# A decoder trunk on one core: stores of tiles that ScalarE wrote last go out from ScalarE's own queue

## The chip, the cores and the metric

The kernel runs on one core of a Trainium2 chip. The metric is the device time of one execution in microseconds, as a median of several executions. A profiled execution has its own time, and the span of its trace runs from the first instruction to the last.

## The reference, cut to what matters

One layer of a decoder for 2048 tokens of width 1024. A mixer whose one input projection is split between a gated linear attention group (GLA, 4 heads) and an RWKV-7 group (8 heads with a recurrent state), one output projection, and then a gated MLP with a causal convolution:

```python
h = modulate(x, norm_mix_g[l], sh_m, sc_m)
proj = h @ w_proj
o_gla = gla_group(proj[..., :GLA_COLS], ...)
o_rwkv, v_first = rwkv7_group(proj[..., GLA_COLS:], ...)
mixed = jnp.concatenate([o_gla, o_rwkv], axis=-1) @ w_out[l]
x = x + gt_m[:, None, :] * mixed
h = modulate(x, norm_ffn_g[l], sh_f, sc_f)
x = x + gt_f[:, None, :] * conv_ffn(h, ffn_up[l], ffn_conv_w[l], ffn_conv_b[l], ffn_down[l])
return rms_norm(x, final_g)
```

## The kernel before

Tokens are cut into 4 blocks of 512. Everything is float32, and a large product is made of three passes over operands split into a high and a low part (`hi`, `lo`): that is what lines 281 to 283, 352 to 354 and 450 to 452 do.

The **first part** of the program (to about 1410 us) is the mixer. Two streams of work are interleaved in it. One is the recurrence, 16 units of 128 tokens: `rwkv_p` prepares a unit, `rwkv_i` and `rwkv_j` invert a small triangular matrix, `rwkv_s` advances the state in two steps, `gla` does the other head group. In a step PE multiplies (L991), ScalarE copies the result out of PSUM to `p1s` (L994), PE multiplies (L999), ScalarE copies to `rw_uv` (L1002), PE multiplies again (L1009). The other stream is filler: `stage_b` makes the input projection of the next block, and `spare` makes the output projection. It gives PE something to do while the recurrence waits.

The **second part** is the MLP, a long run of products (L1268 to L1270 and L1325 to L1327). No transfer of it is touched.

The order on each engine's queue is not the order of the code. The framework schedules the recorded instructions against its own model of their durations, by priority, and then fixes one in-order stream for each engine: PE, DVE, ACT, POOL and SP. Every transfer takes one of eight completion semaphores in turn (`DMAHW0` to `DMAHW7`), over all queues together, and waits until the transfer that had it before, eight transfers earlier, has landed. So a new issuing queue changes what the scheduler does with all five streams.

Transfers to DRAM in the first part, all of them issued by SP before:

- `Weights` (L197 to L202): a weight half is loaded to `w_st`, ScalarE casts it to `w_hi` (L190), DVE or POOL forms `w_lo` (L193). Both are kept in DRAM as `khi` and `klo`, and loaded again for later blocks (L179).
- `evacuate` (L328 to L339): ScalarE copies a projection from PSUM to `ev`; for t of TZ and above, DVE and POOL then add the shifted tokens, and ScalarE saves the last column in `carry` (L338), which is also the last read of the PSUM bank. L339 stores `ev` in `proj`. There are two banks (`g_bank`) for the filler.
- `values_tok` (L360), the branch for TZ (L389) and block 0's first tiles (L587, L589) store tiles that ScalarE copied.
- `rwkv_p` (L864): ScalarE writes `rw_mab` (L855), which goes to DRAM as `inv_a` and comes back in another layout as `rw_ln` (L866) for DVE in `rwkv_i`.

Of the kernel before, what the change touches and what calls it, by code (L numbers as in the profile page):

```python
# [9 lines left out]
F32 = mybir.dt.float32  # L10
# [19 lines left out]
TQ, TK, TV, TG, TZ, TR, TRK, TRV, TWA, TPG = 0, 2, 4, 8, 12, 13, 17, 21, 25, 26  # L30
# [65 lines left out]
def hybrid_kernel(ctx, tc, x, cst, vec, c_row, ada_t, w_in, w_v, w_first, w_z, gk_up, wa_up, g_up,  # L96
                  w_out, ffn_up, ffn_down, out, T=2048):
# [68 lines left out]
    class Weights:  # L166

        def __init__(self, src, split=True, cols=1024, key=None, at=0, keep=True):
            n = pools["np"]
            step = 1024 // n  # L170
            self.step = step
            self.st, self.hi, self.lo = [], [], []
            for i in range((cols + step - 1) // step):
                w = min(step, cols - i * step)
                if split and (key, at + i) in kept:
                    pair = []
                    for s_, from_ in zip(("hi", "lo"), kept[key, at + i]):
                        t = pools["w"].tile([P, step], F32R, name="w_" + s_, tag="w" + s_, bufs=pools["nhl"])
                        nc.sync.dma_start(out=t.bitcast(F32), in_=from_)  # L179
                        pair.append(t)  # L180
                    self.hi.append(pair[0])
                    self.lo.append(pair[1])
                    continue
                t = pools["w"].tile([P, step], F32, name="w_st", tag="wst", bufs=pools["nst"])
                nc.sync.dma_start(out=t[:, 0:w], in_=src[:, i * step:i * step + w])
                self.st.append(t)
                if split:
                    hi = pools["w"].tile([P, step], F32R, name="w_hi", tag="whi", bufs=pools["nhl"])
                    lo = pools["w"].tile([P, step], F32R, name="w_lo", tag="wlo", bufs=pools["nhl"])
                    A.copy(out=hi[:, 0:w], in_=t[:, 0:w])  # L190
                    split_n[0] += 1
                    eng = G if split_n[0] % 3 == 0 else V
                    eng.tensor_tensor(out=lo[:, 0:w], in0=t[:, 0:w], in1=hi[:, 0:w].bitcast(F32), op=ALU.subtract)  # L193
                    self.hi.append(hi)
                    self.lo.append(lo)
                    if key is not None and keep:
                        to = []  # L197
                        for s_, t in (("hi", hi), ("lo", lo)):
                            d_ = dram.tile([P, step], F32, name=f"k{s_}_{len(kept)}")
                            nc.sync.dma_start(out=d_, in_=t.bitcast(F32))  # L200
                            to.append(d_)
                        kept[key, at + i] = to  # L202

# [89 lines left out]
    def dst_of(b, t):  # L293
        for t0, n in groups:
            if t0 <= t < t0 + n:
                return pd[b][t0][:, t - t0, :]
# [31 lines left out]
    def evacuate(b, t, ps):  # L328
        ev = ap.tile([P, NB], F32, name="ev", tag="ev", bufs=pools["nev"])
        if t < TZ:  # L330
            A.activation(out=ev, in_=ps, func=AF.Copy, scale=0.125 if t < TK else 1.0)
        else:

            m = t - TR
            A.activation(out=ev, in_=ps, func=AF.Copy, scale=omu[:, m:m + 1])
            V.scalar_tensor_tensor(out=ev[:, 1:NB], in0=ps[:, 0:NB - 1], scalar=vcol("mu", m), in1=ev[:, 1:NB], op0=ALU.mult, op1=ALU.add)
            G.tensor_tensor(out=ev[:, 0:1], in0=ev[:, 0:1], in1=carry[:, m:m + 1], op=ALU.add)
            A.activation(out=carry[:, m:m + 1], in_=ps[:, NB - 1:NB], func=AF.Copy, scale=vcol("mu", m))  # L338
        nc.sync.dma_start(out=dst_of(b, t), in_=ev)  # L339

    def values_tok(b, h, i):

        bks = [gbank(), gbank()]
        for c in range(2):
            w = Weights(w_v[i, c], key=("v", i, c), keep=b + 1 < NBLK)
            parts_ = [(k, t) for k in range(4) for t in range(4)] if c == 0 else [(k, t) for p_ in range(2) for k in range(4) for t in (2 * p_, 2 * p_ + 1)]
            for k, t in parts_:
                tc.cur_priority += step[0] // 4
                wh, wl = w.pair(k * 256, 256)
                hi, lo = (a_[:, t * P:(t + 1) * P] for a_ in h[4 * c + k])  # L350
                o_ = bks[t // 2][:, (t % 2) * 256:(t % 2) * 256 + 256]
                PE.matmul(out=o_, lhsT=hi, rhs=wh, start=c == 0 and k == 0 and t % 2 == 0, stop=False)
                PE.matmul(out=o_, lhsT=lo, rhs=wh, start=False, stop=False)
                PE.matmul(out=o_, lhsT=hi, rhs=wl, start=False, stop=c == 1 and k == 3 and t % 2 == 1)
            if c == 0:
                yield
        for p_ in range(2):
            ev = ap.tile([P, NB], F32, name="ev", tag="ev", bufs=pools["nev"])
            A.copy(out=ev, in_=bks[p_])
            nc.sync.dma_start(out=pd[b][TV][:, 2 * p_:2 * p_ + 2, i * 256:(i + 1) * 256], in_=ev.rearrange("p (t c) -> p t c", t=2))  # L360
        yield

    def stage_b(b):

        h = ahead.pop(b)[1]
        order = ([TZ] + list(range(8, TZ)) if b == 0 else list(range(8)) + [TZ] + list(range(8, TZ))) + [TWA, TPG] + [TR + i for i in range(12)]
        for i_, t in enumerate(order):
            if b + 1 < NBLK:
                if i_ == len(order) - 15:
                    ahead[b + 1] = stats_a(b + 1)  # L370
                if i_ == len(order) - 11:
                    stats_b(b + 1)
                if i_ == len(order) - 7:
                    stage_a(b + 1, range(0, EXTRA))
                if i_ == len(order) - 2:
                    stage_a(b + 1, range(EXTRA, KT))
            if t == TZ:

                ps = gbank()
                w = Weights(w_z, split=False, cols=KT * 32)  # L380
                for i in range(2):
                    for p_ in range(2):
                        for j in range(4):
                            k = 4 * i + j
                            PE.matmul(out=ps[32 * j:32 * j + 32], lhsT=w.cut(w.st, k * 32, 32), rhs=h[k][p_].bitcast(F32),
                                      start=i == 0 and p_ == 0, stop=i == 1 and p_ == 1)
                ev = ap.tile([P, NB], F32, name="ev", tag="ev", bufs=pools["nev"])
                A.activation(out=ev, in_=ps, func=AF.Identity, bias=vcol("zone"))
                nc.sync.dma_start(out=pd[b][TZ][:, 0, :], in_=ev)  # L389
                yield  # L390
                continue
            if TV <= t < TG:
                if (t - TV) % 2 == 0:
                    yield from values_tok(b, h, (t - TV) // 2)
                continue
            if b > 0 and i_ < 2:
                if i_ == 0:
                    bks = pair_gemm(w_in, 0, "in", h, b + 1 < NBLK)
                ps = bks[i_]
            elif b + 1 < NBLK and i_ >= len(order) - 2:  # L400
                if i_ == len(order) - 2:
                    bks = pair_gemm(w_in, t - 1, "in", h, b + 1 < NBLK)
                ps = bks[i_ - len(order) + 2]
            else:
                ps = gbank()
                t_ = t if t < TZ else t - 1
                gemm3(ps, Weights(w_in[t_], key=("in", t_), keep=b + 1 < NBLK), h)
            evacuate(b, t, ps)
            yield

# [169 lines left out]
    for i, t in enumerate((TQ, TK, TV, TV + 2)):  # L580
        hv, t_ = halves(i, "p0")
        dst = pd[0][min(t, TV)]
        o_ = t - min(t, TV)
        for j in range(2):
            A.activation(out=hv[j], in_=banks[2 * i + j], func=AF.Copy, scale=0.125 if t == TQ else 1.0)
            if t_ is None:
                nc.sync.dma_start(out=dst[:, o_ + j], in_=hv[j])  # L587
        if t_ is not None:
            nc.sync.dma_start(out=dst[:, o_:o_ + 2], in_=t_)  # L589
    ahead[0] = (rb, h0)  # L590
    nc.sync.dma_start(out=ct, in_=cst[:, P:c0])

# [177 lines left out]
    def rwkv_p(b, q, n):  # L770
# [90 lines left out]
        md = dram.tile([2, 8, 4 * 1040], F32, name="inv_a", tag="inv_a", bufs=2)  # L861
        ln = ctile([64, 16, 16], F32, name="rw_ln", tag="rw_ln", bufs=1)
        for par in range(2):
            nc.sync.dma_start(out=md[par, :, 0:4096].rearrange("a (p t) -> p a t", t=64), in_=mv[pars[par]])  # L864
        for par in range(2):
            nc.sync.dma_start(out=ln[par * 32:par * 32 + 32],  # L866
                              in_=md[par].rearrange("a (b y) -> (a b) y", b=4)[:, 0:1024].rearrange("l (s t) -> l s t", t=64)[:, :, 0:16])
# [703 lines left out]
```

## Time and profile before

| | |
|---|---|
| median of 3 runs | 2934.18 us (2933.49 to 2939.03) |
| profiled execution | 2927.03 us, span 2925.2 us |
| PE busy | 2751.4 us, 94% of the span |
| DVE, ACT, POOL busy | 71%, 44%, 37% |
| mean granted TensorE clock | 0.961 |
| transfers | 486.91 MB, 166 GB/s on average |

A profiled execution is one execution: its own time stands 7 us below the median of the others. PE is busy nearly all the time, so what matters is the time in which it waits, and the stretches in which the clock granted to it is below 1.00.

### The profile page before, as it was taken

Reading aid. Unit: us, or ns where it says so; the run is one execution under the profiler, and the core shown is the slowest. Engines: PE = TensorE matmul, PEld = TensorE weight load, DVE = VectorE, ACT = ScalarE, POOL = GpSimd, SP = SyncE. Lnnn points to the kernel's source line nnn. Section 1 sums busy time; section 2 is a strip of 40 time slices with the busy share of each in tenths; the row PEclk is TensorE's granted clock in tenths of the full one; section 3 lists DMA queues with packets and bytes.
Section 4 is the critical chain, followed back from the end, with each engine's and each line's share of the span. In section 5 each row is a group of like instructions: output and inputs, shape, how many; then the busy total and the mean of one; then the engine's idle time right before and its main releaser. Section 6 shows DMA issues by size and latency. Waiting matters only on the chain.

```text
span 2925.2 us, 54728 instructions
## 1 busy us (share of the span) xinstructions
PE 2751.4 (94%) x20296; PEld 2229.9 (76%) x20296; DVE 2085.8 (71%) x4103; ACT 1298.4 (44%) x2721; POOL 1088.3 (37%) x1150
## 2 busy tenths in 40 slices
PE   6989999999999999999779999999997999999998
PEld 5767777877787777778557888888776788888887
DVE  8356977656676667886687685776868786685867
ACT  4444345444444446443354353442534444353443
POOL 5213222312221223332456363553436454363541
PEclk9999999999999999889789999999998999999999
DMA  8989945645545566546314425234564624425243
GB/s 287 352 288 312 280 139 178 191 143 159 171 150 154 163 196 206 164 124 213 120 43 162 141 87 166 87 126 149 185 227 144 209 94 129 138 90 162 88 130 110
DMA packets 363532, 486.91 MB, mean 166 GB/s; under 512 B 80769, under 2 KB 153729, under 8 KB 363265
## 3 DMA queue, kind: packets, MB, share of 16 engines
q1 hardware_dynamic: 363264, 483.41, 51.9%
q8 instruction: 160, 2.62, 0.4%
q14 instruction: 108, 0.88, 0.1%
HBM read 342.77 MB, written 140.51 MB: 165 GB/s over the span
## 4 chain that ended last, share of the span: by engine, by line
PE 69%; DVE 13%; DMA 9%; ACT 3%; issue 3%; POOL 2%; SPq 0%; DVEq 0%; POOLq 0%; ACTq 0%
PE g_bank L1270 9%; PE g_bank L1268 9%; PE g_bank L1269 9%; PE g_bank L1325 5%; PE g_bank L1327 5%; PE g_bank L1326 5%; PE g_bank L281 4%; PE g_bank L283 4%; PE g_bank L282 4%; PE gl_bank L698 1%; DMA rw_k<-proj 1%; DMA acc<-acc 1%; PE g_bank L450 1%; DMA w_st<-in_ada_t 1%; PE g_bank L452 1%
## 5 line engine op out<-in xcount | busy, mean ns | idle before, releaser
L1268 PE MATMUL g_bank<-h_hi,w_hi 128*128 128x512 f32 x1232 | 488.0, 396 | 26.6 <-ACT h_hi L1143 14.8
L1269 PE MATMUL g_bank<-h_lo,w_hi 128*128 128x512 f32 x1232 | 487.3, 396 | 12.7 <-DVE h_lo L1165 6.8
L1270 PE MATMUL g_bank<-h_hi,w_lo 128*128 128x512 f32 x1232 | 479.7, 395 | 9.7 <-POOL w_lo L1144 7.8
L1143 ACT CAST w_hi<-w_st 128x512 fp32r<-128x512 f32 (+1 forms) x396 | 238.6, 607 | 487.4 <-PE g_bank L1326 348.4
L1328 DVE SCALAR_TENSOR_TENSOR acc<-g_bank,mod,acc 128x512 f32<-128x512 f32 (+1 forms) x200 | 144.7, 728 | 249.7 <-PE g_bank L1327 230.7
L1144 POOL TENSOR_TENSOR w_lo<-w_st,w_hi 128x512 fp32r<-128x512 f32 x154 | 219.3, 1425 | 241.7 <-ACT w_hi L1143 237.9
L281 PE MATMUL g_bank<-h_hi,w_hi 128*128 128x512 f32 x736 | 299.0, 406 | 8.0 <-DMA w_hi<-khi 3.8
L1268 PEld LDWEIGHTS g_bank<-h_hi,w_hi 128*128 128x128 f32 x1232 | 235.1, 191 | 81.6 <-ACT h_hi L1143 18.0
L282 PE MATMUL g_bank<-h_lo,w_hi 128*128 128x512 f32 x736 | 294.9, 401 | 0.0
L283 PE MATMUL g_bank<-h_hi,w_lo 128*128 128x512 f32 x736 | 294.9, 401 | 0.0
L1269 PEld LDWEIGHTS g_bank<-h_lo,w_hi 128*128 128x128 f32 x1232 | 235.0, 191 | 64.1 <-DVE h_lo L1165 8.2
L1270 PEld LDWEIGHTS g_bank<-h_hi,w_lo 128*128 128x128 f32 x1232 | 234.9, 191 | 63.3 <-POOL w_lo L1144 12.3
L1325 PE MATMUL g_bank<-hh,w_hi 128*128 128x512 f32 x640 | 251.9, 396 | 6.0 <-DVE acc L1328 6.0
L1326 PE MATMUL g_bank<-hl,w_hi 128*128 128x512 f32 x640 | 251.6, 395 | 0.0
L1327 PE MATMUL g_bank<-hh,w_lo 128*128 128x512 f32 x640 | 251.6, 395 | 0.0
L1144 DVE TENSOR_TENSOR w_lo<-w_st,w_hi 128x512 fp32r<-128x512 f32 (+1 forms) x242 | 201.6, 833 | 15.2 <-ACT w_hi L1143 10.5
L281 PEld LDWEIGHTS g_bank<-h_hi,w_hi 128*128 128x128 f32 x736 | 140.3, 191 | 41.6 <-issue 4.5
L283 PEld LDWEIGHTS g_bank<-h_hi,w_lo 128*128 128x128 f32 x736 | 140.1, 190 | 30.8 <-DMA w_lo<-klo 0.7
L282 PEld LDWEIGHTS g_bank<-h_lo,w_hi 128*128 128x128 f32 x736 | 140.6, 191 | 28.0 <-issue 0.2
L1325 PEld LDWEIGHTS g_bank<-hh,w_hi 128*128 128x128 f32 x640 | 120.1, 188 | 37.3 <-DVE acc L1328 6.9
L1327 PEld LDWEIGHTS g_bank<-hh,w_lo 128*128 128x128 f32 x640 | 120.2, 188 | 29.4
L1326 PEld LDWEIGHTS g_bank<-hl,w_hi 128*128 128x128 f32 x640 | 120.2, 188 | 29.1
(342 smaller groups left out, 6108.7 us busy)
## 6 DMA issues: line engine op xcount, KB each, us to landing
acc<-acc SPq DMA_DIRECT2D x352, 256.0 KB, 3.1
w_hi<-khi SPq DMA_DIRECT2D x188, 256.0 KB, 3.5
w_lo<-klo SPq DMA_DIRECT2D x188, 256.0 KB, 3.8
w_st<-in_ffn_up SPq DMA_DIRECT2D x176, 256.0 KB, 2.9
proj<-ev SPq DMA_DIRECT2D x100, 256.0 KB, 3.5
w_st<-in_ffn_down SPq DMA_DIRECT2D x80, 256.0 KB, 2.7
khi<-w_hi SPq DMA_DIRECT2D x68, 256.0 KB, 3.8
klo<-w_lo SPq DMA_DIRECT2D x68, 256.0 KB, 3.9
```

The costliest lines, as they stand in the source:

```text
L281: PE.matmul(out=ps, lhsT=wh, rhs=hi, start=k == 0, stop=False)
L282: PE.matmul(out=ps, lhsT=wh, rhs=lo, start=False, stop=False)
L283: PE.matmul(out=ps, lhsT=wl, rhs=hi, start=False, stop=k == KT - 1)
L1143: A.copy(out=hi, in_=t)
L1144: eng.tensor_tensor(out=lo, in0=t, in1=hi.bitcast(F32), op=ALU.subtract)
L1268: PE.matmul(out=ps, lhsT=wh[:, c], rhs=hi, start=first and k == 0, stop=False, skip_group_check=True)
L1269: PE.matmul(out=ps, lhsT=wh[:, c], rhs=lo, start=False, stop=False, skip_group_check=True)
L1270: PE.matmul(out=ps, lhsT=wl[:, c], rhs=hi, start=False, stop=last and k == 3, skip_group_check=True)
L1325: PE.matmul(out=ps, lhsT=wh, rhs=hh, start=j == 0, stop=False)
L1326: PE.matmul(out=ps, lhsT=wh, rhs=hl, start=False, stop=False)
L1327: PE.matmul(out=ps, lhsT=wl, rhs=hh, start=False, stop=j == n - 1)
L1328: V.scalar_tensor_tensor(out=a_, in0=ps, scalar=mod[:, 40 + ft:41 + ft], in1=a_, op0=ALU.mult, op1=ALU.add)
```

## The change

Of the stores above, 149 are issued from ScalarE's queue: 68 `khi` halves, 28 projections with t below TZ, 12 of `values_tok`, 4 of TZ, 5 first tiles of block 0, and 32 of `inv_a`. SP keeps 68 `klo` halves, 56 projections with t of TZ and above, and all loads. The same bytes go to the same places.

```diff
--- before.py
+++ after.py
@@ -197,7 +197,7 @@
                         to = []
                         for s_, t in (("hi", hi), ("lo", lo)):
                             d_ = dram.tile([P, step], F32, name=f"k{s_}_{len(kept)}")
-                            nc.sync.dma_start(out=d_, in_=t.bitcast(F32))
+                            (A if s_ == "hi" else nc.sync).dma_start(out=d_, in_=t.bitcast(F32))
                             to.append(d_)
                         kept[key, at + i] = to
 
@@ -336,7 +336,7 @@
             V.scalar_tensor_tensor(out=ev[:, 1:NB], in0=ps[:, 0:NB - 1], scalar=vcol("mu", m), in1=ev[:, 1:NB], op0=ALU.mult, op1=ALU.add)
             G.tensor_tensor(out=ev[:, 0:1], in0=ev[:, 0:1], in1=carry[:, m:m + 1], op=ALU.add)
             A.activation(out=carry[:, m:m + 1], in_=ps[:, NB - 1:NB], func=AF.Copy, scale=vcol("mu", m))
-        nc.sync.dma_start(out=dst_of(b, t), in_=ev)
+        (A if t < TZ else nc.sync).dma_start(out=dst_of(b, t), in_=ev)
 
     def values_tok(b, h, i):
 
@@ -357,7 +357,7 @@
         for p_ in range(2):
             ev = ap.tile([P, NB], F32, name="ev", tag="ev", bufs=pools["nev"])
             A.copy(out=ev, in_=bks[p_])
-            nc.sync.dma_start(out=pd[b][TV][:, 2 * p_:2 * p_ + 2, i * 256:(i + 1) * 256], in_=ev.rearrange("p (t c) -> p t c", t=2))
+            A.dma_start(out=pd[b][TV][:, 2 * p_:2 * p_ + 2, i * 256:(i + 1) * 256], in_=ev.rearrange("p (t c) -> p t c", t=2))
         yield
 
     def stage_b(b):
@@ -386,7 +386,7 @@
                                       start=i == 0 and p_ == 0, stop=i == 1 and p_ == 1)
                 ev = ap.tile([P, NB], F32, name="ev", tag="ev", bufs=pools["nev"])
                 A.activation(out=ev, in_=ps, func=AF.Identity, bias=vcol("zone"))
-                nc.sync.dma_start(out=pd[b][TZ][:, 0, :], in_=ev)
+                A.dma_start(out=pd[b][TZ][:, 0, :], in_=ev)
                 yield
                 continue
             if TV <= t < TG:
@@ -584,9 +584,9 @@
         for j in range(2):
             A.activation(out=hv[j], in_=banks[2 * i + j], func=AF.Copy, scale=0.125 if t == TQ else 1.0)
             if t_ is None:
-                nc.sync.dma_start(out=dst[:, o_ + j], in_=hv[j])
+                A.dma_start(out=dst[:, o_ + j], in_=hv[j])
         if t_ is not None:
-            nc.sync.dma_start(out=dst[:, o_:o_ + 2], in_=t_)
+            A.dma_start(out=dst[:, o_:o_ + 2], in_=t_)
     ahead[0] = (rb, h0)
     nc.sync.dma_start(out=ct, in_=cst[:, P:c0])
 
@@ -861,7 +861,7 @@
         md = dram.tile([2, 8, 4 * 1040], F32, name="inv_a", tag="inv_a", bufs=2)
         ln = ctile([64, 16, 16], F32, name="rw_ln", tag="rw_ln", bufs=1)
         for par in range(2):
-            nc.sync.dma_start(out=md[par, :, 0:4096].rearrange("a (p t) -> p a t", t=64), in_=mv[pars[par]])
+            A.dma_start(out=md[par, :, 0:4096].rearrange("a (p t) -> p a t", t=64), in_=mv[pars[par]])
         for par in range(2):
             nc.sync.dma_start(out=ln[par * 32:par * 32 + 32],
                               in_=md[par].rearrange("a (b y) -> (a b) y", b=4)[:, 0:1024].rearrange("l (s t) -> l s t", t=64)[:, :, 0:16])
```

The scheduler then orders all engines anew. Three places show what that looks like.

The **sync queue**, where a unit's `inv_a` goes out while the filler loads kept weights (`w_hi<-khi`, `w_lo<-klo`). Before:

```order
L780 DMA rw_pg<-proj_26_100 128x128
L339 DMA proj_26_110<-ev 128x512
L1047 DMA mix_113<-rw_yq 128x4x128
L864 DMA inv_a<-rw_mab 64x8x64 x2
L866 DMA rw_ln<-inv_a 32x16x16 x2
L179 DMA w_hi<-khi_1191 128x512
L179 DMA w_lo<-klo_1193 128x512
```

With the change:

```order
L780 DMA rw_pg<-proj_26_100 128x128
L339 DMA proj_26_110<-ev 128x512
L1047 DMA mix_113<-rw_yq 128x4x128
L866 DMA rw_ln<-inv_a 32x16x16
L179 DMA w_hi<-khi_1191 128x512
L866 DMA rw_ln<-inv_a 32x16x16
L179 DMA w_lo<-klo_1193 128x512
```

The two stores are gone; the two loads of `rw_ln`, which need them landed, keep their places among the loads of weights.

**ScalarE**, about where the last projections of block 0 are evacuated and block 1's first weights are cast (`w_hi_1812` and `w_hi_1822` are the same halves in both). Before:

```order
L338 ACTIVATE carry_137<-g_bank_1453,vt_66 128x1
L190 CAST w_hi_1812<-w_st_1810 128x512
L190 CAST w_hi_1822<-w_st_1820 128x512
L682 COPY gl_kt_3010<-gl_bank_3011 128x256
L335 ACTIVATE ev_1549<-g_bank_1504,omu_139 128x512
L338 ACTIVATE carry_137<-g_bank_1504,vt_66 128x1
```

With the change:

```order
L338 ACTIVATE carry_137<-g_bank_1453,vt_66 128x1
L190 CAST w_hi_1812<-w_st_1810 128x512
L200 DMA khi_36_1816<-w_hi_1812 128x512
L704 COPY atf_658<-gl_bank_3108 64x64
L705 COPY atf_658<-atd0_659 64x2x64
L706 COPY atf_658<-atd0_659 64x2x64
L190 CAST w_hi_1822<-w_st_1820 128x512
L335 ACTIVATE ev_1549<-g_bank_1504,omu_139 128x512
L200 DMA khi_37_1826<-w_hi_1822 128x512
L338 ACTIVATE carry_137<-g_bank_1504,vt_66 128x1
```

A store now stands behind each cast, and `khi_37` stands between the copy `ev_1549` and the `carry` that ends the reading of its bank.

**PE**, in one step of the recurrence near its end (`rs_bank_14603` is written by L999, and L1009 needs ScalarE's copy of it in `rw_uv`). Before:

```order
L281 MATMUL g_bank_14182<-h_hi_13632,w_hi_14195 128x512
L282 MATMUL g_bank_14182<-h_lo_13633,w_hi_14195 128x512
L999 MATMUL rs_bank_14603<-p1s_656,yf1_655 64x64 x4
L690 MATMUL gl_bank_14417<-gl_d_14261 32x32 x2
L698 MATMUL gl_bank_14417<-gl_d_14261 64x64 x10
L698 MATMUL gl_bank_14417<-gl_qk_14163 64x64 x2
L699 MATMUL gl_bank_14417<-gl_d_14261 64x64
L999 MATMUL rs_bank_14603<-p1s_656,yf1_655 64x64 x4
L283 MATMUL g_bank_14182<-h_hi_13632,w_lo_14196 128x512
L281 MATMUL g_bank_14182<-h_hi_13638,w_hi_14195 128x512
```

33 more rows stand there before L1009 of that step, 17 of them of L281 to L283. With the change:

```order
L452 MATMUL g_bank_13651<-h_hi_13644,w_lo_13700 128x512
L450 MATMUL g_bank_13652<-h_hi_13644,w_hi_13709 128x512
L451 MATMUL g_bank_13652<-h_lo_13645,w_hi_13709 128x512
L452 MATMUL g_bank_13652<-h_hi_13644,w_lo_13710 128x512
L999 MATMUL rs_bank_14603<-p1s_656,yf1_655 64x64 x8
L1009 MATMUL rs_bank_14614<-rw_uv_14569,rw_bkt_13149 64x64 x8
L851 MATMUL rp_bank_14058<-rw_t_14040,rw_bk_14041 128x128 x4
L852 MATMUL rp_bank_14059<-rw_t_14040,rw_bk_14041 128x128 x4
```

L1009 follows L999 at once.

## Rows read from the trace of the kernel before

**Rows 1.** Page, part 1: busy time of each engine, us (share of span), instructions.
```profile
PE 2751.4 (94%) x20296; PEld 2229.9 (76%) x20296; DVE 2085.8 (71%) x4103; ACT 1298.4 (44%) x2721; POOL 1088.3 (37%) x1150
```

**Rows 2.** Windows: each engine's busy us (instructions), granted clock, DMA share, GB/s.
```profile
0.00:1440.00 1440.00, 1340.98 (x14130) 1082.71 (x14130) 984.51 (x2723) 663.73 (x1656) 397.67 (x516) 0.95 0.64 201
...
200.00:420.00 220.00, 195.37 (x1885) 160.56 (x1883) 170.42 (x489) 91.75 (x229) 61.43 (x68) 0.92 0.81 258
...
1100.00:1300.00 200.00, 187.51 (x2111) 150.52 (x2102) 163.53 (x467) 102.20 (x273) 67.12 (x83) 0.87 0.54 166
...
1410.00:1500.00 90.00, 49.05 (x216) 35.70 (x216) 70.42 (x85) 38.16 (x64) 52.85 (x41) 0.70 0.29 88
```

**Rows 3.** Page, part 4: the chain that ended last, by engine.
```profile
PE 69%; DVE 13%; DMA 9%; ACT 3%; issue 3%; POOL 2%; SPq 0%; DVEq 0%; POOLq 0%; ACTq 0%
```

**Rows 4.** Waits of the sync queue, 0 to 1440 us: total us, times, longest.
```profile
SPq L179 <- PE g_bank L283: 130.0, 72, 12.9
...
SPq L864 <- ACT rw_mab L855: 39.4, 14, 7.8
...
SPq L200 <- ACT w_hi L190: 26.7, 22, 3.2
...
SPq L866 <- DMA inv_a<-rw_mab: 22.7, 21, 2.8
...
SPq L360 <- ACT ev L359: 12.5, 6, 5.2
...
SPq L339 <- ACT ev L331: 8.2, 8, 2.2
...
SPq L200 <- ACT atf L704: 6.6, 3, 2.9
```

**Rows 5.** Waits of PE, 0 to 1440 us: total us, times, longest.
```profile
PE g_bank L450 <- ACT carry L338: 12.3, 3, 8.3
...
PE rs_bank L1009 <- ACT rw_uv L1002: 2.4, 1, 2.4
...
PE rp_bank L113 <- DMA rw_v<-proj: 1.2, 2, 0.6
```

**Rows 6.** Issues of the stores by line: ns minimum/median/maximum, first and last start.
```profile
L200 SPq DMA_DIRECT2D khi<-w_hi x68: 319/382/1697, 71.8 to 1170.2; - x68
...
L339 SPq DMA_DIRECT2D proj<-ev x84: 319/332/1227, 94.1 to 1097.0; - x84
...
L360 SPq DMA_DIRECT2D proj<-ev x12: 370/374/992, 264.7 to 894.5; - x12
...
L589 SPq DMA_DIRECT2D proj<-p x3: 407/821/1006, 77.0 to 81.4; - x3
...
L864 SPq DMA_DIRECT2D inv_a<-rw_mab x32: 595/615/625, 269.2 to 1324.2; - x32
```

**Rows 7.** Timeline, ACT then PE, 207 to 213 us: start, us, instruction [idle before].
```profile
207.72 1.27 ACT L335 ACTIVATE ev<-g_bank,omu 128x512 f32<-128x512 f32 x2
212.19 0.62 ACT L190 CAST w_hi<-w_st 128x512 fp32r<-128x512 f32 x1 [3.20 <-DMA w_st<-in_w_in]
212.71 0.41 ACT L338 ACTIVATE carry<-g_bank,vt 128x1 f32<-128x1 f32 x2
...
213.02 0.79 PE L450 MATMUL g_bank<-h_hi,w_hi 128*128 128x512 f32 x1 [8.28 <-ACT carry L338]
```

**Rows 8.** Timeline, ACT then PE, about 1403 us.
```profile
1403.77 0.75 ACT L1002 COPY rw_uv<-rs_bank 64x256 f32<-64x256 f32 x2 [4.43 <-PE rs_bank L999]
...
1403.04 0.69 PE L999 MATMUL rs_bank<-p1s,yf 128*64 128x64 f32 x16
...
1403.99 0.39 PE L450 MATMUL g_bank<-h_hi,w_hi 128*128 128x512 f32 x1
1404.22 0.40 PE L451 MATMUL g_bank<-h_lo,w_hi 128*128 128x512 f32 x1
```

## Prediction

> **What bounds the kernel now.** I read the page from the top. The share of busy time [rows 1] comes first: TensorE (PE) works in 94% of the span, ScalarE in 44%. A change that touches neither the number nor the length of matmuls can only move PE's idle time and the clock it is granted. The chain that ended last [rows 3] says who stands between matmuls: VectorE 13%, transfers 9%, ScalarE 3%, and the sync engine's own queue (SPq) 0%. So the issuing of transfers is nowhere on the path as a whole.
>
> Next the windows [rows 2], since the change is in the first part alone. Over 0 to 1440 us PE is idle for 99.0 us (1440 less 1341.0). Three stretches hold most of what can move: 200 to 420 us, where the transfers are dense (DMA share 0.81) and PE idles 24.6 us at clock 0.92; 1100 to 1300 us, 12.5 us idle at 0.87; and the passage to the second part, 1410 to 1500 us, 41.0 us idle at 0.70. A clock of 0.87 over 200 us means work of 26 us lost to the lower of the two levels (13% of 200), so that stretch loses 38.5 us in all.
>
> Then the waits of the two queues that the change touches. SP [rows 4] waits longest for PE (130.0 us at L179, a reload of weights that needs a free buffer), which the change leaves alone. For ScalarE's tiles, ahead of stores that now leave SP, it waits 39.4 us at L864, 26.7 and 6.6 us at L200, 12.5 us at L360 and 8.2 us at L339: 93.4 us. PE's own waits [rows 5] say whether that hurts: for a load it waits 1.2 us at L113; for ScalarE 12.3 us, three times, at L450 (a bank that `carry` has not finished reading) and 2.4 us once at L1009. In 1440 us PE hardly waits for a late transfer, and does wait for a late ScalarE.
>
> **What the change removes, adds and moves.** 149 issues move from SP to ScalarE; bytes and destinations stay.
>
> *Term A, issuing on ScalarE.* The price of an issue is taken from SP's rows [rows 6], since before ScalarE issues none of these stores: 68 `khi` at 0.382 us make 26.0; 28 + 4 at 0.332 (L339's form) 10.6; 12 at 0.374 4.5; 5 at 0.821 4.1; 32 `inv_a` at 0.615 19.7. That adds 64.9 us to ScalarE's queue, 5% to its 1298.4 us. It is nothing if all of it lies in ScalarE's idle time (it works 663.7 of the first 1440 us), and 64.9 us if ScalarE is always what PE waits for. The nearest row is ScalarE's share of the chain: 3% of 2925.2 us is 88 us, 6.8% of its 1298.4 busy us. I price the issues alike: 64.9 x 0.068 = **+4.4 us**. Queued behind them are the evacuations (L331 to L338, L359), the casts and the copies to `p1s` and `rw_uv`; PE waits for all of these.
>
> *Term B, relief of SP.* Not all 93.4 us of waits vanish. Behind each `khi` stands `klo`, made from `w_hi` by another engine later, so SP waits there for it instead; behind `inv_a` stands the load of `rw_ln`, which needs the store landed (L866 waits 22.7 us for it already [rows 4]). What goes for good is L360 and L339, 20.7 us, and the issue time. Bounds: 0, since the queue has 0% of the chain and PE waits 1.2 us for such loads, to -20.7. I stay near the chain's row and take **-2 us**.
>
> The Trainium skill, DMA: Bandwidth & Descriptors, section "Issuing engines are not separate DMA queues", says that transfers started by any engine run on the same 16 DMA engines, and that spreading the issuing saves only the sequencer's time, usually small. By it B would be 0 and the sum below 2 us higher. The DMA share of 0.81 in 200 to 420 us [rows 2] agrees that the shared part is what is loaded there.
>
> *Term C, shorter cover in the recurrence.* The order is made anew. Between L999 and L1009 stands a ScalarE copy; [rows 8] show its length: L999 starts at 1403.04 and takes 0.69, the copies start at 1403.77 and end 0.75 later, 0.79 us after L999's end, or about 1.0 us after its last matmul's start. Meanwhile PE needs other work, at 0.23 us a big matmul (1403.99 to 1404.22). Counting the work between such pairs over all 16 units, the order before falls short of 1.0 us once, by 0.1 us. With the change L1009 falls short six times, with 0.7, 0.8, 0.6, 0.2, 0.2 and 0.5 us of cover, and L999 once behind `p1s`, with 0.9: 3.0 + 0.1 = 3.1 us. Less the 0.1 of before, **+3 us**; 0 if the streams are elsewhere late enough to hide it, 6 if the clock falls to the lower level in these gaps and doubles it.
>
> *Term D, the passage to the second part.* With the change the last step of the recurrence, some 4 us of small products, is mixed with the first matmuls of the MLP (L1268), where before the last projection matmuls covered it. That is work for a stretch with 41.0 us of idle PE [rows 2], but VectorE, busy 70.4 of its 90 us, has that step's work to do as well. Bounds -4 and +4 by those 4 us; I take **-1 us**.
>
> *Clock and the spread of filler.* The filler matmuls between successive units move: from unit 12 on, 103, 119 and 105 stand between one L880 and the next, where it was 93, 74 and 73. I set this at 0 in the sum, since more filler there means less elsewhere, and treat it as a rival.
>
> **Sum:** 4.4 - 2 + 3 - 1 = +4.4 us on the profiled 2927.0 us, so 2931.4. That execution stands 7 us below the median of the runs, so the difference is carried to the median: 2934.2 + 4 = **2938 us**. A measurement of this kernel tells about 0.2%, 5.9 us, from nothing, so this forecast is near its own limit of detection.
>
> **Rivals.**
>
> *1. ScalarE's queue blocks in order (slower).* In front of each store the queue must wait until its completion semaphore, used eight transfers earlier, is free, and on ScalarE everything behind waits too. [rows 7] show what one such hold costs: a cast waits 3.20 us for `w_st`, the `carry` behind it is late, and PE stands idle for 8.28 us and goes on at 0.79 us a matmul, where 0.39 is the rule [rows 8]. With the change `khi` stores stand at just this place, and about half of the 68 fall before 420 us. In the other direction, SP's issue of `khi` took up to 1.697 us against a median of 0.382 [rows 6]. If two more holds of that size arise, 16.6 us take the place of the 4.4 of term A, and the sum is +16.6: about 2951 us. It decides from one hold on, if it is longer than the filler in the second bank; holds that stay under a tile of matmuls (24 at 0.23, 5.5 us) cost nothing. Against it: only three waits at L450 in 1440 us.
>
> *2. The new order fills 1100 to 1300 us better (faster).* That stretch loses 38.5 us; with a third more filler between its units (327 matmuls in place of 240), a third of the loss, 13 us, may go: 4.4 - 13 = -8.6, about 2925 us. Against it: the filler is taken from somewhere, and the same total of matmuls is done.
>
> *3. Nothing happens.* The issues lie in ScalarE's idle time, SP's waits move to `klo` and `rw_ln`, and the reordering evens out: 2934 us. For it: 0% of SPq, 1.2 us of waits for loads. The rule of the Trainium skill named above would end here as well.
>
> **Chances.** The forecast 0.40, with a range of its own of 2931 to 2945; blocked ScalarE 0.22; better filler 0.23; nothing 0.15. Faster by over 0.2% comes from the better filler (0.21) and a little of the third (0.04): 0.25. Slower comes from the blocked queue (0.20), 0.16 of the forecast and 0.01 of the third: 0.37. The rest, 0.38, is the same. The range runs from the bound of B on top of the second rival's side, some 15 us below the median, to the first rival and a little more of term A: 2919 to 2957 us.
>
> **What the changed profile would show.** Term A: rows of issues on ScalarE's queue near the prices above, and PE's waits for `carry` and `rw_uv` a few us longer than 12.3 and 2.4. If the first rival holds, they are tens of us, in 200 to 420 us, with more idle PE there than 24.6 us. Term B: SP's waits for ScalarE at L360 and L339 gone, and others at L200 (for `klo`) and L866 grown by about what L864 and `khi` lose. Term C: small waits of PE at L1009 and L999. Term D: idle PE in 1410 to 1500 us near 41 us. The second rival: PE's idle time and the clock in 1100 to 1300 us against 12.5 and 0.87. The prediction is wrong if PE's idle time or its mean clock moves by much in a stretch where none of the terms has a place, for the order of the whole first part is new.

## The result, and the profile after

The changed kernel takes 2916.44 us (median of 8 runs, 2911.54 to 2929.59), the kernel before 2933.84 us in the 8 runs beside it. The ratio is 0.9949, 95% interval 0.9934 to 0.9963: **faster by 0.5%**, some 15 us by the ratio (the two medians stand 17 us apart). Forecast were 2938 us and a range of 2919 to 2957; the time lies below it, on the side that had a chance of 0.25.

The profiled execution has 2920.9 us, a span of 2918.8. It stands 4 us above its median and that of before 7 us below, so the two traces differ by 6 us where the medians differ by 17. Traces of single stretches are therefore compared below with further ones of the same order.

Part 1 of the page, and the chain that ended last, by engine:

```profile
PE 2746.2 (94%) x20296; PEld 2224.0 (76%) x20296; DVE 2080.9 (71%) x4103; ACT 1303.1 (45%) x2721; POOL 1083.5 (37%) x1150
...
PE 58%; DVE 10%; DMA 6%; issue 2%; ACT 2%; POOL 2%; SPq 0%; DVEq 0%; ACTq 0%; POOLq 0%
```

ACTq, the queue that now issues 149 stores, has 0% of the chain, as SPq had [rows 3]. The windows answer to [rows 2]:

```profile
0.00:1440.00 1440.00, 1339.34 (x14136) 1080.07 (x14136) 989.89 (x2727) 671.07 (x1660) 402.11 (x517) 0.95 0.64 202
...
200.00:420.00 220.00, 203.04 (x1827) 166.86 (x1825) 162.61 (x452) 93.89 (x235) 59.64 (x67) 0.90 0.81 267
...
1100.00:1300.00 200.00, 185.86 (x2172) 150.21 (x2172) 161.57 (x460) 100.16 (x267) 68.76 (x82) 0.92 0.59 179
...
1410.00:1500.00 90.00, 56.15 (x302) 42.10 (x303) 69.61 (x90) 42.28 (x73) 50.57 (x42) 0.75 0.23 74
```

In 200 to 420 us PE idles 17.0 us where it idled 24.6, at a lower clock; in 1100 to 1300 us it idles 14.1 in place of 12.5, at 0.92 in place of 0.87; in 1410 to 1500 us 33.9 in place of 41.0. Nothing says yet whether the queue or the order did that.

Issues of the stores by line (ns minimum, median, maximum; first and last start), beside [rows 6]:

```profile
L200 ACTq DMA_DIRECT2D khi<-w_hi x68: 326/326/814, 72.3 to 1171.9; - x68
...
L339 ACTq DMA_DIRECT2D proj<-ev x28: 326/326/792, 92.8 to 948.3; - x28
...
L360 ACTq DMA_DIRECT2D proj<-ev x12: 366/377/415, 268.4 to 894.4; - x12
...
L589 ACTq DMA_DIRECT2D proj<-p x3: 327/1083/1097, 77.4 to 80.1; - x3
...
L864 ACTq DMA_DIRECT2D inv_a<-rw_mab x32: 582/597/1027, 278.8 to 1337.2; - x32
```

The issues cost on ScalarE's queue about what they cost on SP's. SP's waits, 0 to 1440 us, beside [rows 4]:

```profile
SPq L179 <- PE g_bank L283: 98.3, 60, 7.4
SPq L866 <- DMA inv_a<-rw_mab: 62.8, 18, 9.9
...
SPq L200 <- DVE w_lo L193: 24.4, 18, 3.4
...
SPq L200 <- POOL w_lo L193: 22.4, 10, 10.7
```

The waits for ScalarE at L864, L200, L360 and L339 are gone, and others have taken their place: L866 waits 62.8 us for `inv_a` to land (22.7 before), and L200 waits for the engines that form `w_lo`, the tile stored in `klo`. PE's waits, 0 to 1440 us, beside [rows 5]:

```profile
PE gl_bank L113 <- DVE gl_o L737: 8.1, 2, 7.8
...
PE rs_bank L1009 <- ACT rw_uv L1002: 3.1, 4, 1.1
...
PE g_bank L450 <- ACT carry L338: 2.6, 2, 2.0
...
PE rs_bank L999 <- ACT p1s L994: 1.9, 2, 1.0
```

The wait of 8.28 us for `carry` at 207 us is not there; in its place PE waits 7.8 us for `gl_o`.

### The profile page after: what moved, and what is told of

Read it like the earlier page. It is cut to its first block, busy times and chain, and to the rows that moved or that the text cites. A ratio compares the mean times of both kernels' runs of the same rounds, so it can differ in the third digit from the quotient of the medians.

```text
span 2918.8 us, 54644 instructions
## 1 busy us (share of the span) xinstructions
PE 2746.2 (94%) x20296; PEld 2224.0 (76%) x20296; DVE 2080.9 (71%) x4103; ACT 1303.1 (45%) x2721; POOL 1083.5 (37%) x1150
## 4 chain that ended last, share of the span: by engine, by line
PE 58%; DVE 10%; DMA 6%; issue 2%; ACT 2%; POOL 2%; SPq 0%; DVEq 0%; ACTq 0%; POOLq 0%
PE g_bank L1270 9%; PE g_bank L1268 9%; PE g_bank L1269 9%; PE g_bank L1325 5%; PE g_bank L1327 5%; PE g_bank L1326 5%; PE g_bank L281 3%; PE g_bank L282 3%; PE g_bank L283 3%; DVE rw_pr L901 1%; DMA rw_k<-proj 1%; DMA acc<-acc 1%; PE gl_bank L698 1%; DMA rw_ln<-inv_a 1%; POOL w_lo L1144 1%
## 5 line engine op out<-in xcount | busy, mean ns | idle before, releaser
L1268 PE MATMUL g_bank<-h_hi,w_hi 128*128 128x512 f32 x1232 | 486.9, 396 | 28.1 <-ACT h_hi L1143 17.2
L281 PE MATMUL g_bank<-h_hi,w_hi 128*128 128x512 f32 x736 | 298.4, 406 | 7.6 <-DMA w_hi<-khi 5.7
L1268 PEld LDWEIGHTS g_bank<-h_hi,w_hi 128*128 128x128 f32 x1232 | 234.8, 191 | 82.4 <-ACT h_hi L1143 20.0
L283 PE MATMUL g_bank<-h_hi,w_lo 128*128 128x512 f32 x736 | 293.3, 399 | 0.1
L1270 PEld LDWEIGHTS g_bank<-h_hi,w_lo 128*128 128x128 f32 x1232 | 234.0, 190 | 61.0 <-POOL w_lo L1144 12.4
L281 PEld LDWEIGHTS g_bank<-h_hi,w_hi 128*128 128x128 f32 x736 | 139.5, 190 | 41.4 <-DMA w_hi<-khi 3.0
L283 PEld LDWEIGHTS g_bank<-h_hi,w_lo 128*128 128x128 f32 x736 | 139.3, 189 | 30.7 <-DMA w_lo<-klo 0.8
```

What stands on the lines that cost most here:

```text
L281: PE.matmul(out=ps, lhsT=wh, rhs=hi, start=k == 0, stop=False)
L283: PE.matmul(out=ps, lhsT=wl, rhs=hi, start=False, stop=k == KT - 1)
L1268: PE.matmul(out=ps, lhsT=wh[:, c], rhs=hi, start=first and k == 0, stop=False, skip_group_check=True)
L1270: PE.matmul(out=ps, lhsT=wl[:, c], rhs=hi, start=False, stop=last and k == 3, skip_group_check=True)
```

## The experiments

An edit that moves stores to another queue changes two things, the queue and the scheduler's order of all five streams. The first experiments take them apart. The program is traced and scheduled twice: once with the stores on the queues that `ORDER` names, to read off the order of every engine, and once more with the queues of `RUN`, with each instruction tied behind the one that stood before it on its engine. The tie is meant to set the order of issue alone. No run has the tie by itself. But each of the two orders was also run without it ("both again" and "the kernel before, again"), and queue and tie together move the ratio by less than 0.001. Only the moved stores are left to find their places. The cut below is that of the order alone; for the queue alone the values of `ORDER` and `RUN` are exchanged:

```diff
+ORDER = ('khi', 'ev', 'v', 'p', 'inv')
+RUN = ()
...
+            for name, engine in follow:
+                i = here.get(name)
+                if i is None or str(i.engine) != engine:
+                    continue
+                if str(i.engine) in last:
+                    tc.add_manual_dep(i, last[str(i.engine)], mybir.DependencyInfo(mybir.DependencyClass.NoSync, mybir.DependencyReason.DATA), reason="order")
+                last[str(i.engine)] = name
```

**Order alone** (changed order, all stores on SP).

> The five engines keep the order that the changed kernel has, instruction by instruction, but the 149 stores are issued by the sync engine again. If the new order brings the gain (theory O), this is faster than before by about the whole 17 us, ratio 0.994 to 0.996, since the order of PE, VectorE and GpSimd is that of the changed kernel. If the queue itself brings it (theory Q), it is within 4 us of before, ratio 0.999 to 1.001. My term B put at most 2 us on the queue, so I hold with O.

Measured: 2915.42 us, ratio 0.9926 (0.9912 to 0.9941). All of the gain is there with no store moved.

**Queue alone** (order of before, 149 stores on ScalarE).

> All engines keep the order of the kernel before, and only the 149 stores go out from ScalarE's queue. Theory O: no gain, and 0 to 4 us slower by the issues (term A less term B), ratio 1.000 to 1.002. Theory Q: faster by about 17 us, ratio 0.994 to 0.996. Were the first rival at work (ScalarE held by a store), it would be slower by 8 us or more, ratio above 1.003.

Measured: 2941.13 us, ratio 1.0011 (0.9997 to 1.0026). No gain. Q and the first rival fall. PE's waits in this trace:

```profile
PE g_bank L450 <- ACT carry L338: 10.3, 3, 6.1
```

The kernel before, run again (below), has this row to the digit: the stores in ScalarE's queue made no `carry` later. SP's queue shows that the wait for a landed store did grow:

```profile
SPq L866 <- DMA inv_a<-rw_mab: 71.0, 25, 10.2
```

**Both again**, the changed kernel in the form that the other two are made from.

> The changed kernel once more, in the form that the other two are made from: its order and its queues. Ratio 0.993 to 0.997 by every theory; its trace is a second one of the changed kernel. A ratio above 0.998 would mean that the measured gain was for the most part chance.

Measured: 2917.13 us, ratio 0.9935 (0.9917 to 0.9954), with no tie. The gain was not chance between executions.

**An order that nobody chose**:

```diff
-    filler, lag = [None], [370]
+    filler, lag = [None], [372]
```

> The kernel before with one number of its filler's priority changed (lag 372 where it was 370), all stores on the sync engine: a new order that nobody meant to be better. If an order picked at random moves the time by as much as the change did (theory O in its weak form, chance), the ratio is away from 1 by 0.003 or more in either direction. If the order before is about as good as its neighbours, and the changed kernel's order is better for a reason of its own, it lies within 0.002 of 1.

Measured: 2931.69 us, ratio 0.9985 (0.9972 to 0.9999). This one other order is worth 0.15%, less than the 0.3% that would have made the gain ordinary, though not nothing. It happens to share the changed kernel's end: 103, 119 and 105 filler matmuls stand between the units 12 to 15 in its trace, and that spread alone does not bring the gain.

Next, where in the order it lies. The pinned order is now spliced: up to L880 of a chosen unit from the one kernel, the rest in the other's, stores on SP:

```diff
+def spliced(first, then):
+    at = [name for name, _ in first].index(CUT)
+    done = {name for name, _ in first[:at]}
+    return first[:at] + [(n, e) for n, e in then if n not in done]
```

**New order from unit 11 on.**

> All stores on the sync engine. Up to L880 of the unit 11 (about 1047 us, where both orders have done the same filler) every engine keeps the order of the kernel before; from there the order of the changed kernel. Aligned by matmul work done, the new order won most where the units 13 to 15 run (about 13 us), 2 us in the passage to the second part, and lost 3 between. Theory L (the late spread of filler is the cause): ratio 0.994 to 0.997, 10 to 17 us. Rival E (the early part, the blocks 0 to 2, is the cause): within 0.002 of 1.

Measured: 2935.34 us, ratio 0.9989 (0.9974 to 1.0004). My theory L falls, as far as it said that the net gain comes from the end.

**New order up to unit 11.**

> The complement: the changed kernel's order up to L880 of the unit 11, then that of the kernel before; all stores on the sync engine. Theory L: 0 to 5 us faster, ratio 0.998 to 1.000. Rival E: 0.994 to 0.996. If both are additive, this ratio and that of the late splice multiply to that of the order alone, 0.993.

Measured: 2918.31 us, ratio 0.9938 (0.9918 to 0.9957). Most of the gain is here, and the two ratios multiply to 0.9927, that of the order alone.

**The late rate**, a spread of the end made by one number in the source:

```diff
-                rate[0] = 0.55
+                rate[0] = 0.75
```

> The kernel before, with one number changed: the rate at which filler is asked for in the last block, 0.75 for 0.55. Up to the unit 12 the order is that of before; then 122, 79, 119 filler matmuls stand between the units 12 to 15 and 164 after, where it was 93, 74, 73 and 242. All stores on the sync engine. Theory L says that the spread is what counts, whoever makes it: ratio 0.994 to 0.998. If the gain is a matter of other details of the changed kernel's order, it is within 0.002 of 1.

Measured: 2916.7 us, ratio 0.9937 (0.9917 to 0.9956). So the end does have 18 us to give, though the changed kernel's end did not give them.

**All stores on ScalarE** (order of before pinned; `klo` and the projections from TZ on moved as well).

> Every engine keeps the order of before, and now klo and the projections from TZ on go out from ScalarE's queue as well: 273 stores, 124 of them of tiles that VectorE or GpSimd finished. The issue price of terms A and B alone would make 1.8 times what the 149 cost with the same order (0.0011, some 3 us): ratio 1.001 to 1.003. If a store held in ScalarE's queue by another engine's result blocks the evacuations behind it (first rival), it is slower by 15 us or more, ratio above 1.005.

Measured: 2950.37 us, ratio 1.005 (1.0032 to 1.0068), on the border between the two readings. It costs about 15 us. PE's waits for ScalarE in this trace sum over the first 1440 us to 51.5, against 48.8 with the 149 stores, so no large block shows. Where the time goes in this trace is read under "Stretch by stretch".

**Both gains together**: new order up to unit 11, from there the order that rate 0.75 gives.

> Up to L880 of the unit 11 the changed kernel's order, from there the order that the rate 0.75 gives; all stores on the sync engine. Early order alone gave 0.9938, the rate alone 0.9937. If the two gains come from different stretches (theory S, several stretches) they add: ratio 0.986 to 0.990, some 36 us. If both runs were faster by one common cause, the ratio stays at 0.992 to 0.995.

Measured: 2905.86 us, ratio 0.99 (0.9878 to 0.9921), the fastest version found, 31 us below the kernel before. Its ratio lies at the upper end of the first expectation and a little above the product 0.9875: the gains add for the most part.

**New order up to unit 1, 4 and 7** tell which part of the early order gains.

> The changed kernel's order only up to L880 of the unit 1 (about 336 us), then that of before; all stores on the sync engine. PE's wait of 6 to 8 us for carry at about 207 us is then gone. If the part up to unit 1 carries the early gain, ratio 0.993 to 0.996; by the loss aligned by work (9 us less at 250 us of work) I expect 0.996 to 0.998.

Measured: 2942.48 us, ratio 1.0022 (1.0005 to 1.0038): no gain, if anything slower, a miss. That PE no longer waits 6 to 8 us for `carry` at 207 us gains nothing by itself: PE waits 6.8 us for `gl_o` instead.

> The changed kernel's order up to L880 of the unit 7 (about 758 us), then that of before; all stores on the sync engine. By the loss aligned by work the gain of the early part, some 12 us, is complete there: ratio 0.994 to 0.997. If it lies between the units 7 and 11, the ratio is above 0.998.

Measured: 2927.32 us, ratio 0.9968 (0.9957 to 0.9979). Half of the gain.

> The changed kernel's order up to L880 of the unit 4, then that of before; all stores on the sync engine. 140, 144 and 139 filler matmuls then stand before the units 2, 3 and 4. If the spread over these units is the cause of the early gain, it is there in full: ratio 0.995 to 0.998. If it lies in the units 5 to 7, the ratio is above 0.999.

Measured: 2933.95 us, ratio 0.9994 (0.9984 to 1.0004): no net gain yet, and the condition that I had set against the spread over the units 2 to 4 is met. What its trace adds is read under "Stretch by stretch".

**The kernel before, again.**

> The kernel before with its own order and queues, in the form that the spliced kernels are made from. Ratio 0.998 to 1.002: what is away from 1 here is chance, and no reading of less may be built on. Its trace is a second one of the kernel before; the first came from an execution of 2927.0 us, 7 below the median, and I expect some 5 to 10 us more loss in the first 500 us.

Measured: 2938.28 us, ratio 1.0008 (0.9995 to 1.0021). Ratios within about 0.001 of 1 are not told from chance. Its trace is 13 us longer than the first one of before; 5 us of that lie ahead of the 97th L1268 matmul (1572 against 1567 us) and 8 behind it, not in the first 500 us as I had expected.

**An even spread by two numbers** (rate 0.9 for 0.85 up to block 2, and 0.75 for 0.55 at the end), and **another order by two** (lag 340 for 370, and 0.75 for 0.55).

> The kernel before with two numbers changed: filler rate 0.9 for 0.85 in the blocks 0 to 2, and 0.75 for 0.55 in the last. 169, 119, 99 filler matmuls before the units 2 to 4, and 113, 121, 126, 137 at the end, the most even end of all. If an even spread is the cause in both places, ratio 0.986 to 0.992, as the spliced best (0.990) or better. If only the changed kernel's own early order gains, it is that of the late rate alone, 0.992 to 0.996, or worse.

Measured: 2941.51 us, ratio 1.0017 (1.0003 to 1.0031). A miss: the most even end of all makes the kernel no faster, if anything slower.

> The kernel before with lag 340 for 370 and rate 0.75 for 0.55 in the last block. The units 2 to 4 have 130, 95 and 169 filler matmuls, so the stretch up to unit 3 is that of before, and the end has 99, 120, 107, 169, much like the changed kernel's 103, 119, 105, 180. By the spread: the gain of the end less what the unit 12 (181 for 210) gives back, ratio 0.994 to 0.998.

Measured: 2918.82 us, ratio 0.9946 (0.9934 to 0.9958), as expected.

**Stretch by stretch.** Below are the windows from L880 of unit 1 to that of unit 7, 11, 12 and 15, and from there to the 97th L1268 matmul in the MLP, at the times where each trace has them. First the kernel before, again (columns as in [rows 2]; the DVE, ACT and POOL figures don't matter here):

```profile
327.00:759.00 432.00, 408.06 (x4931) 330.12 (x4918) 302.20 (x904) 197.16 (x516) 109.15 (x156) 0.95 0.57 173
759.00:1050.00 291.00, 282.49 (x3310) 227.36 (x3309) 193.32 (x591) 133.98 (x357) 59.77 (x100) 0.98 0.53 160
1050.00:1158.00 108.00, 100.49 (x1149) 78.81 (x1147) 73.08 (x215) 56.51 (x154) 29.58 (x40) 0.98 0.67 214
1158.00:1331.00 173.00, 163.30 (x1986) 132.46 (x1986) 142.56 (x404) 87.30 (x225) 57.88 (x72) 0.86 0.48 142
1331.00:1572.00 241.00, 197.91 (x1373) 155.46 (x1372) 158.71 (x272) 90.86 (x179) 95.18 (x85) 0.89 0.45 143
```

The order alone:

```profile
333.00:751.00 418.00, 404.77 (x4906) 327.55 (x4905) 303.84 (x880) 192.81 (x494) 105.18 (x153) 0.94 0.56 171
751.00:1036.00 285.00, 275.81 (x3266) 223.75 (x3267) 188.88 (x579) 134.71 (x356) 60.05 (x98) 0.98 0.54 163
1036.00:1144.00 108.00, 97.92 (x1077) 77.84 (x1073) 69.83 (x201) 53.31 (x137) 24.59 (x39) 0.89 0.60 189
1144.00:1334.00 190.00, 176.82 (x2152) 142.87 (x2150) 152.15 (x441) 99.06 (x257) 72.06 (x79) 0.94 0.57 171
1334.00:1554.00 220.00, 177.61 (x1278) 139.67 (x1275) 147.43 (x253) 83.88 (x164) 90.60 (x82) 0.89 0.42 135
```

The late rate, from unit 11 on, the stretches before it being those of before:

```profile
1051.00:1158.00 107.00, 100.08 (x1148) 78.65 (x1147) 73.06 (x214) 56.75 (x154) 29.77 (x40) 0.97 0.68 215
1158.00:1340.00 182.00, 170.16 (x2061) 135.85 (x2060) 148.42 (x416) 93.42 (x234) 63.68 (x75) 0.93 0.55 168
1340.00:1555.00 215.00, 173.57 (x1297) 136.26 (x1296) 152.74 (x261) 84.41 (x168) 92.98 (x83) 0.90 0.42 134
```

The even spread:

```profile
326.00:772.00 446.00, 426.09 (x4919) 342.07 (x4918) 308.47 (x910) 199.02 (x521) 104.28 (x157) 0.93 0.55 169
772.00:1075.00 303.00, 295.82 (x3357) 236.72 (x3356) 196.95 (x594) 136.65 (x364) 63.12 (x100) 0.97 0.55 163
1075.00:1168.00 93.00, 80.04 (x927) 64.02 (x926) 67.96 (x190) 48.44 (x123) 27.73 (x36) 0.88 0.61 195
1168.00:1364.00 196.00, 185.06 (x2232) 148.30 (x2231) 153.65 (x435) 100.10 (x257) 66.56 (x79) 0.95 0.57 173
1364.00:1575.00 211.00, 171.76 (x1290) 133.33 (x1289) 150.60 (x262) 83.63 (x168) 89.97 (x81) 0.88 0.40 126
```

The stretches hold different amounts of filler, so their lengths don't compare; what is lost in them does. Loss is the idle time of PE, plus the length times what the clock lacks to 1.00 (in the first row 23.9 + 0.05 x 432 = 45.5). The clock has two digits, so each figure is good to some 2 us, and time in which PE idles at a lower clock counts in both parts:

| us lost in units | 1 to 7 | 7 to 11 | 11 to 12 | 12 to 15 | 15 to the MLP | sum |
|---|---|---|---|---|---|---|
| before, again | 45.5 | 14.3 | 9.7 | 33.9 | 69.6 | 173.0 |
| order alone | 38.3 | 14.9 | 22.0 | 24.6 | 66.6 | 166.4 |
| late rate 0.75 | as before | as before | 10.1 | 24.6 | 62.9 | |
| even spread | 51.1 | 16.3 | 24.1 | 20.7 | 64.6 | 176.8 |

The order of the changed kernel loses 9 us less in the units 12 to 15, as the second rival had it, and pays 12 us for it in the unit 11 to 12, from which the filler was taken (188 matmuls in place of 210 before the unit 12; the late rate leaves 208 there and keeps the gain). What stays is the 7 us of the units 1 to 7, where PE idles 13.2 us in place of 23.9, and smaller ones that two-digit clocks don't resolve. The even spread shows the same trade at its worst: 13 us won in the units 12 to 15, 14 lost in the unit 11 to 12, 6 lost in the units 1 to 7.

The changed kernel itself loses 39.5 us in the units 1 to 7, 21.6 in the unit 11 to 12 and 28.8 in the units 12 to 15, the same pattern, and in the units 7 to 11 less, 6.7 us idle at 0.99, or 9.5 us:

```profile
758.00:1039.00 281.00, 274.31 (x3287) 222.91 (x3282) 190.06 (x582) 135.33 (x358) 61.95 (x99) 0.99 0.56 166
```

The table explains 7 of the 24 us between its first two traces. Ahead of unit 1 lie 3.5 more (38.8 us idle against 35.3), and behind the passage some 7, where both have nearly the same order: that part is taken as chance between two executions. The remainder is in no row: PE counts as busy there, with modelled ends of its matmuls. Firmer than any two traces are the splices, each over several runs: new order up to unit 1, 4, 7, 11 and throughout makes 1.0022, 0.9994, 0.9968, 0.9938 and 0.9926, so the net gain has come by unit 11.

That the splices at units 1 and 4 show none of it does not mean that the new order gains nothing there. Where a splice joins, its order is that of neither kernel: the splice at unit 4 has 139 filler matmuls between the units 3 and 4, where the new order has 104 and that of before 229. In the units 1 to 7 its trace loses 49.7 us, more than that of before:

```profile
334.00:757.00 423.00, 398.66 (x4853) 323.50 (x4851) 301.63 (x872) 192.20 (x494) 104.69 (x153) 0.94 0.56 169
```

Reckoned in the same way, the six traces that keep the order of before up to unit 11 (before, again, queue alone, all stores on ScalarE, new order from unit 11 on, late rate) and the five that keep the new one (changed kernel, both again, order alone, new order up to unit 11, both gains together) compare so:

| us lost, mean (range) | start to unit 1 | units 1 to 7 | units 7 to 11 |
|---|---|---|---|
| order of before | 52.8 (51.9 to 54.1) | 46.1 (43.9 to 48.1) | 15.4 (12.4 to 21.3) |
| new order | 49.0 (47.3 to 52.8) | 39.2 (38.3 to 40.3) | 10.5 (7.4 to 14.9) |

The new order loses some 4, 7 and 5 us less, 16 in all, near the 18 us of the splice at unit 11. Only in the units 1 to 7 do the ranges stand apart. No single long wait makes it there: the longest of PE's is 3.9 us in the kernel before, again, and 3.8 us with the order alone.

The same reckoning places what all 273 stores on ScalarE cost. From unit 11 on its trace has:

```profile
1052.00:1168.00 116.00, 108.10 (x1152) 84.69 (x1151) 74.38 (x215) 58.31 (x155) 28.92 (x41) 0.91 0.63 200
1168.00:1342.00 174.00, 162.59 (x1987) 131.69 (x1986) 142.59 (x402) 86.25 (x222) 57.83 (x72) 0.86 0.46 140
1342.00:1587.00 245.00, 201.40 (x1375) 157.94 (x1374) 160.37 (x275) 91.89 (x181) 96.33 (x85) 0.87 0.45 143
```

That is 18.3, 35.8 and 75.5 us lost, 16 more than in the kernel before, again, in the same stretches and the same order of PE. Nearly 14 of the 16 are clock (0.91 against 0.98 in the first of them) and under 3 are idle time, so PE's list of waits does not show them. It is one trace, and why the clock falls there is not shown.

## Why the prediction was wrong

The step that failed is the one under "Clock and the spread of filler": "I set this at 0 in the sum, since more filler there means less elsewhere". The new order alone, with no store moved, is worth -0.74% (0.9912 to 0.9941), some -22 us, more than all the other terms together. I had the order of all five streams before me and priced it at two places, the short cover of seven hops (+3) and the passage to the second part (-1); the rest I left at nothing because I could not tell its sign. What the runs showed in its place is less idle time and lost clock ahead of unit 11, some 16 us by the traces and 18 by the splice. The new order was not made for that: that it is better than the old one is luck as far as the idea of the change goes.

The lower end of the range, 2919 us, does not follow from its own sentence: 15 us below the median is the bound of B alone (-20.7 in place of -2 makes the sum -14.3). Put on top of the second rival's -8.6, as the sentence says, it makes -27, or about 2907 us. The measured time lies above that, but for neither of the two reasons: the queue alone gained nothing, and the second rival's gain was given back.

*Term A*'s prices of an issue held. They were 0.382, 0.332, 0.374, 0.821 and 0.615 us; measured are 0.326, 0.326, 0.377, 1.083 and 0.597, and the 149 issues sum to 63.4 us where 64.9 were forecast. With *term B* it makes +2.4 us; the queue alone measured +0.0011, 3.2 us, with an interval from -0.9 to 7.6, and order alone against both again (0.9926 and 0.9935) points the same way, though neither is told from zero. The sum of A and B stands within that; its parts, and the share of 0.068 by which A was priced, were not measured singly.

*Term B*'s mechanism held. In the changed kernel L360 and L339 wait no more for ScalarE, `klo` and `rw_ln` wait instead, and none of it moved the time: with the queue alone L866 waits 71.0 us in place of 22.7 [rows 4], and nothing is gained. The rule of the Trainium skill (DMA: Bandwidth & Descriptors, section "Issuing engines are not separate DMA queues") says that only the issue time is saved, and the runs agree: moving 149 issues off SP gained nothing that can be measured.

*Term C* was about right: PE waits 3.1 us at L1009, four times, and 1.9 at L999, twice; of before I know 2.4 [rows 5] and, in its list of waits, 0.6. That is +2.0 where I had +3.

*Term D* was small as forecast: after unit 15 PE idles 42.4 us with the new order and 43.1 with that of before. The 7 us less in the window 1410 to 1500 us [rows 2] come mostly from a window at fixed times.

*The first rival* (a store that blocks ScalarE) did not occur with these stores, although more of them stood where it was feared than the prediction says: 52 of the 68 `khi` stores start before 420 us in the trace before, not about half. [rows 7] showed a wait for `carry` behind a late transfer, and I had taken stores at that place for more of it; they changed no such wait. *The second rival* had the right cause, the order, and the right stretch, and still not the reason of the gain: its 9 us came, and were given back one unit earlier. The half of my own objection that "the filler is taken from somewhere" was right there; it was wrong in that other stretches gained too.

What stays open: which detail of the early order gains. It lies ahead of unit 11, and by the traces in more than one stretch, most clearly in the units 1 to 7. The spread of filler over the units 2 to 4 was my candidate. The splice at unit 4, with 140, 144 and 139, and the even spread lose 49.7 and 51.1 us in the units 1 to 7, where the new order loses 38 to 40, and both speak against it. A splice has an order of its own where its halves meet, so its place is known to about a unit.

## What to carry to other kernels

Where a scheduler orders all engines anew, an edit is two edits. Build the old queue with the new order and the new queue with the old order before anything is said of the edit: here the idea measured +0.1% in time (-0.03% to +0.26%), no gain, and its side effect -0.7%. What an order does must not be put at zero because its sign is unknown; it belongs in the range, with the losses of idle time and clock in the stretches it touches as its size. And once the order is known to be worth that much, turn it directly: one number (the late rate) gained as much as the change, and with the early order of the changed kernel it makes 0.99. Other orders made by one or two numbers came out between 0.9946 and 1.0017, so each has to be measured.

## What the runs showed of the hardware that was not expected

An issue on ScalarE's queue can overlap with its arithmetic. Timeline of the changed kernel, ScalarE and its queue:

```profile
144.69 0.20 ACT L704 COPY atf<-gl_bank 64x64 f32<-64x64 f32 x1
144.79 0.30 ACT L705 COPY atf<-atd 64x128 f32<-64x128 f32 x1
144.82 0.33 ACTq L200 DMA_DIRECT2D khi<-w_hi  x1
145.10 0.30 ACT L706 COPY atf<-atd 64x128 f32<-64x128 f32 x1
```

The issue runs from 144.82 to 145.15; the copy of 144.79 runs beside it, and the next copy starts at 145.10, as that copy has ended and before the issue has. Of the 149 issues in this trace 64 begin while an instruction of ScalarE executes, 13 see another one start before they have ended, and some 23 of their 63.4 us lie beside such work. So 63 us of issues are less than 63 us of ScalarE's time. That may be one reason why the queue alone cost only some 3 us; no run separates it from the idle time of ScalarE into which other issues fall.
